# Projections of a hybrid trunk in plain float32 instead of float32r products of split operands, with a ring of 8 weight tiles

## The chip, the cores and the metric

The kernel runs on one NeuronCore of a Trainium2 chip, alone. The metric is the device time of one execution in microseconds (us). Before the change three timed executions took 1420.29, 1420.82 and 1422.03 us; the median is 1420.82 us. The engines are named as the profile names them: PE is TensorE (PEld its weight loads), DVE is VectorE, ACT is ScalarE, POOL is GpSimd, SP is SyncE, which here does little but issue DMAs.

## The reference

One layer on 256 tokens of width 1024, float32 throughout:

```
mod = silu(c) @ ada_w + ada_b                     # 6 x 1024: shift, scale, gate, twice
h   = rmsnorm(x) * (1 + scale1) + shift1
proj = h @ w_in                                   # 1024 x 6688
gdn = 8 heads of a chunked gated delta rule on conv + silu of proj columns, gated, normed
ssd = 16 heads of a chunked state-space scan on conv + silu of proj columns, gated, normed
x   = x + gate1 * (concat(gdn, ssd) @ w_out)      # 2048 x 1024
h   = rmsnorm(x) * (1 + scale2) + shift2
x   = x + gate2 * moe(h)                          # top 4 of 32 experts, each 1024 -> 2 x 1024 -> 1024
out = rmsnorm(x) * final_g
```

## The kernel before

The program has two parts. The **front** does everything up to the router: the vectors of ada_w, the input projection, the delta-rule heads in four pairs (`gdn_pair`), the state-space heads (`ssd`), the output projection, the router. The **expert part** then streams all weights of the 32 experts, 12 loads of 1 MB each, through 20 tiles of 1 MB (`SLOTS`, one tag each; load number n of the stream goes into tag n modulo 20).

In the front the same 20 tiles carry other data. Some are working memory (tags such as g, s1, even, xT), and five, w0 to w4, are the **ring** of weights (`RING`). A unit of the ring is 1 MB: 256 columns of w_in (`Win`, 26 units, the first two before the main loop), 512 columns by 512 rows of w_out (`Wout`, 8 units, which use three tags) or 256 columns of ada_w (`Ada`, 24 units). `issue(tag)` puts the next load into SyncE's queue when its tag is released; loads go in one fixed order and one queue. As the ring empties, `Early` units and `fetch` put the first expert loads into freed tags in the same queue, ahead of later w_out units.

A Win or Wout unit is two **jobs** (`Job`), each 128 columns of w_in (8 products of a 128x128 stationary tile with 256 moving columns, one per 128 rows of depth) or two depth tiles of w_out (4 products of a 128x128 stationary tile with 512 moving columns). A product is not one matmul. `Job.split` first makes a float32r copy of the weights on ACT (`whs`, L323) and the remainder on POOL (`wls`, L327, two halves per job; for the first two units on DVE), one job ahead. The activations are kept as such a pair too (`hs`; for the output projection `ys`, split at L1007 and L1172 on ACT and L1008 and L1173 on DVE). Three float32r matmuls then stand for the float32 product: high x high, high x low, low x high (L363 for Win, L449 for Wout). The weight tile is released right after the split.

A Win job's result lies in one of two PSUM banks of tag mm, from which the convolution reads it: one ACT operation (L538), three DVE operations (L540), then a tanh on ACT and a last DVE operation. The bank is free after the third L540. An Ada unit of the main loop is a chain of eight DVE operations on 128x256 elements (L390, L392). A generator, `fill`, hands out the jobs in halves; `run` mixes those halves into the 27 steps of each `gdn_pair` and the 26 of `ssd`, so that PE has projection work while the heads wait for DVE or ACT. Each engine works through its queue in order.

Chores (loads of biases and of ada_b rows) are issued by POOL, each pinned behind a POOL subtraction of a split.

Of the kernel before, what the change touches and what calls it, by code (L numbers as in the profile page):

```python
# [16 lines left out]
try:  # L17
# [15 lines left out]
KT = D // 128  # L33
# [15 lines left out]
def trunk_kernel(ctx: ExitStack, tc: tile.TileContext, x, c, ada_w, ada_b, norm1_g, norm2_g, w_in,  # L49
# [20 lines left out]
    def slot(tag, name, dt=FT, size=2048):  # L70
        return ring.tile([128, size], dt, name=name, tag=tag, bufs=1)
# [40 lines left out]
    def ts(t):  # L112
        return slice(t * 128, t * 128 + 128)
# [37 lines left out]
    BC = part("s3", 0, [4, SEQ])  # L151
    whs, wls = slot("wh", "whs", FR), slot("wl", "wls", FR)
    nth = {}
# [158 lines left out]
    class Job:  # L312
# [4 lines left out]

        def split(self, dst=None):
            u, i = self.unit, self.i
            w = u.half(i)  # L320
            h = turn("wh") * 1024
            self.wh, self.wl = (v[:, h:h + 1024] for v in dst or (whs, wls))
            self.first = S.activation(u.shaped(self.wh), w, AF.Copy)  # L323
            wh, wl = u.shaped(self.wh), u.shaped(self.wl)
            q = w.shape[1] // 2
            for r in (slice(0, q), slice(q, 2 * q)):
                self.last = (V if dst else G).tensor_tensor(wl[:, r], w[:, r], wh[:, r], op=OP.subtract)  # L327
            if i:
                u.w = None
                issue(u.tag)  # L330

        def mm(self, part):
            self.unit.mm(self, part)

        def post(self):
            self.unit.post(self)

    class Win:
# [8 lines left out]

        def half(self, i):
            return self.w[:, :, ts(i)]

        def shaped(self, v):
            return v.rearrange("p (k m) -> p k m", k=KT)

# [5 lines left out]
        def mm_k(self, job, ks):  # L359
            wh, wl = self.shaped(job.wh), self.shaped(job.wl)  # L360
# [59 lines left out]
    class Wout:  # L420
# [8 lines left out]

        def half(self, i):  # L430
            return self.w[:, 2 * i:2 * i + 2]

        def shaped(self, v):
            return v.rearrange("p (k m) -> p k m", k=2)

        def mm(self, job, t):
            wh, wl = self.shaped(job.wh), self.shaped(job.wl)
# [13 lines left out]

# [22 lines left out]
    def fill():  # L474

        todo, sums, late = None, [], []
        jobs = [j for u in units[KT + 2:] if not isinstance(u, Early) for j in (u.jobs or [u])]
        real = [None] * 4 + [j for j in jobs if isinstance(j, Job)]
        real[4].split()
        n = 4  # L480

        def between():
            if sums:
                try:
                    next(sums[0][0])
                except StopIteration:
                    late.append([1, sums.pop(0)[1]])

        for j in jobs:
            if isinstance(j, Ada):  # L490
                sums.append((j.run(False), j))
# [11 lines left out]
            if n < len(real):  # L503
                real[n].split()
            if n >= 6 and n % 2 == 0 and chores:
                with tc.issue_after(real[n].last.ins):
# [104 lines left out]
    for i, u in enumerate(units[KT:], KT):  # L611
        u.tag = f"w{((i if i < w0 else w0 + (i - w0) % 3) - KT) % RING}"
    for u, i in zip(units, (4, 2, 1, 3, 4, 2, 3, 4)):
        u.tag = f"w{i}"
# [5 lines left out]
    xh = slot("yh", "xh").rearrange("p (t d) -> p t d", t=2)  # L620
    hT = slot("yl", "hT").rearrange("p (k m) -> p k m", k=KT)
    ss1 = fc.tile([128, 2], FT)
# [10 lines left out]

    hs = [slot(tag, "hs", FR).rearrange("p (k m) -> p k m", k=KT) for tag in ("hh", "hl")]
# [5 lines left out]
    wx = [slot(tag, "wx", FR) for tag in ("s2", "g")]  # L640

    def pre_run(i, k):

        for j in pre[2 * i:2 * i + 2]:
            if j.k == 0:
                j.split(wx if i else (whs, wls))
        for j in pre[2 * i:2 * i + 2]:
            j.unit.mm_k(j, range(j.k, k))
            j.k = k

    for k2 in range(KT // 2):
# [70 lines left out]
    wbx = slot("xd", "wbh", FR)  # L722
    wbh = wbx[:, 0:512].rearrange("p (a k m) -> p a k m", a=2, k=KT)
    with tc.issue_after(last[0].ins):
        S.activation(wbh[:, 0], wbd, AF.Copy)
    with tc.issue_after(last[1].ins):
        V.tensor_tensor(wbh[:, 1], wbd, wbh[:, 0], op=OP.subtract)
    p = pg()
    for k in range(KT):
        for j, (a, b) in enumerate(((0, 0), (0, 1), (1, 0))):  # L730
            T.matmul(p[0:32, :SEQ], wbh[:, a, k], hs[b][:, k], start=(k == 0 and j == 0), stop=(k == KT - 1 and j == 2))
    bd = fr.tile([32, 4, 2, 64], FT, name="bd", tag="rot", bufs=3)
# [84 lines left out]
    def gdn_pair(pr):  # L817
# [211 lines left out]
    def gate_chore(dst, c0):  # L1029
        chores.append(lambda: nc.gpsimd.dma_start(dst, ada_b[:, c0:c0 + dst.shape[1]].to_broadcast(list(dst.shape))))  # L1030

    def bias_load(i, src):
        chores.append(lambda: nc.gpsimd.dma_start(bf[32 * i:32 * i + 32], src))

# [31 lines left out]
    def ssd():  # L1066
# [44 lines left out]
        for qd in range(4):  # L1111
# [42 lines left out]
            if qd % 2:  # L1154
# [10 lines left out]
                for t in range(2):  # L1165
                    T.transpose(p[:, ts(t)], rsd[:, t:t + 1].to_broadcast([128, 128]), ident)
                parts_y()
                for ct in range(4 * g, 4 * g + 4):
                    V.scalar_tensor_tensor(xT[:, ct], xT[:, ct], sng[:, ct:ct + 1], p[:, 0:256],
                                           op0=OP.mult, op1=OP.mult)  # L1170
                    yhl = ys[2 + g][:, :, ct % 4]
                    S.activation(yhl[:, 0], xT[:, ct], AF.Copy)  # L1172
                    V.tensor_tensor(yhl[:, 1], xT[:, ct], yhl[:, 0], op=OP.subtract)  # L1173
                yield


    ys = []

    def parts_y():
        ys.append(slot(("yh", "yl")[len(ys) % 2], "ys", FR).rearrange("p (a k m) -> p a k m", a=2, k=4))  # L1180

    parts_y()
    parts_y()
# [405 lines left out]
```

## Time and profile before

| | us |
|---|---|
| median of three timed executions | 1420.82 |
| profiled execution, its own time | 1424.03 |
| its span, first to last instruction | 1422.2 |

The span lies 1.8 us inside the profiled execution's time, and that execution took 3.2 us longer than the median. In the rows further down a busy time is the union of an engine's instructions in a stretch; PEclk is the mean clock that was granted to PE, as a share of full speed (1.00 is 2.4 GHz, 0.50 is 1.2 GHz). A plain float32 matmul of the program stands in the trace as two MATMUL records, a float32r matmul as one. The ends of matmul records are modelled and overlap the next record, so a pace is read from starts and not from durations.

### The profile page before, as it was taken

To read this page: it belongs to the slowest core of one execution; us is meant where nothing else is said; L and a number is where in the kernel's file an instruction comes from. 1 tells how busy PE (TensorE), PEld (TensorE's weight loads), DVE (VectorE), ACT (ScalarE), POOL (GpSimd) and SP (SyncE) were. 2 spreads that over 40 slices of the span, in tenths; PEclk is the share of its full clock that TensorE was granted. 3 is DMA by queue.
4 is the path that set the end of the run, shared out by engine and by line. 5 is a ranking of instruction groups with operands and counts; after the bars stand their busy time and mean duration, and the time that the engine had idled before them with its cause. 6 is when DMAs were issued, how large, how long until landed. Compare 5 with 4: busy or idle time off the path is not lost. (4 is left out here: it accounts for less than half of the span.)

```text
span 1422.2 us, 20287 instructions
## 1 busy us (share of the span) xinstructions
PE 1272.2 (89%) x8024; PEld 662.7 (47%) x8025; DVE 627.0 (44%) x1586; ACT 246.4 (17%) x464; POOL 210.3 (15%) x185
## 2 busy tenths in 40 slices
PE   5889698889888899999999999899998799999996
PEld 3777687788666333333333323233333333333332
DVE  6889998954686322323322322223222133222322
ACT  3343333342243000001000000001000010100001
POOL 3345443444464000000000000000000000000000
PEclk8989898999999999999999999999999899999997
DMA  9754455332628699999999999999999999999990
GB/s 340 240 168 162 155 159 177 110 129 86 240 90 319 276 424 423 422 424 424 424 423 422 424 424 423 423 423 424 424 424 424 424 424 424 381 423 424 422 409 33
DMA packets 130472, 469.78 MB, mean 330 GB/s; under 512 B 7900, under 2 KB 59216, under 8 KB 97568
## 3 DMA queue, kind: packets, MB, share of 16 engines
q1 hardware_dynamic: 128592, 464.58, 81.3%
q8 instruction: 95, 1.56, 0.4%
q0 software_dynamic: 1040, 1.67, 0.4%
q10 hardware_dynamic: 704, 1.64, 0.4%
q14 instruction: 41, 0.34, 0.1%
HBM read 466.22 MB, written 1.05 MB: 329 GB/s over the span
## 5 line engine op out<-in xcount | busy, mean ns | idle before, releaser
L1398 PE MATMUL pG<-w,xe 128*64 128x512 f32 (+1 forms) x1152 | 283.5, 579 | 21.3 <-DMA w<-in_moe_w_gu_dram 21.1
L1398 PE MATMUL pU<-w,xe 128*64 128x512 f32 (+1 forms) x1152 | 280.6, 574 | 0.0
L1426 PE MATMUL pY<-w,hTe 128*64 128x512 f32 x1024 | 225.2, 592 | 0.9 <-ACT hTe L1415 0.7
L1402 DVE TENSOR_SCALAR ga<-pG 128x512 f32<-128x512 f32 (+1 forms) x34 | 23.0, 676 | 411.8 <-PE pG L1398 411.8
L327 POOL TENSOR_TENSOR wls<-w,whs 128x512 fp32r<-128x512 f32 x128 | 170.0, 1350 | 216.5 <-ACT whs L323 205.8
L363 PE MATMUL mm<-hs,whs 128*128 128x256 f32 x800 | 174.1, 310 | 30.7 <-DVE t_c L540 13.1
L1398 PEld LDWEIGHTS pG<-w,xe 128*64 128x64 f32 (+1 forms) x1152 | 83.9, 135 | 163.1 <-issue 103.9
L1398 PEld LDWEIGHTS pU<-w,xe 128*64 128x64 f32 (+1 forms) x1152 | 87.9, 135 | 142.4 <-issue 139.9
L363 PEld LDWEIGHTS mm<-hs,whs 128*128 128x128 f32 x800 | 136.5, 207 | 37.7 <-issue 24.4
L1426 PEld LDWEIGHTS pY<-w,hTe 128*64 128x64 f32 x1024 | 71.8, 137 | 133.0 <-issue 127.9
L363 PE MATMUL mm<-hs,wls 128*128 128x256 f32 x400 | 121.8, 304 | 0.0
L1404 ACT ACTIVATE th<-ga 128x512 f32<-128x512 f32 (+1 forms) x34 | 21.1, 620 | 470.4 <-DVE ga L1402 470.4
L1437 DVE SCALAR_TENSOR_TENSOR ye<-pY,gs,g2p 128x512 f32<-128x512 f32 (+1 forms) x33 | 24.2, 734 | 172.7 <-PEq L1491 163.8
L323 ACT ACTIVATE whs<-w 128x1024 fp32r<-128x1024 f32 x66 | 69.8, 1058 | 84.6 <-PE mm L363 41.7
L363 PEld LDWEIGHTS mm<-hs,wls 128*128 128x128 f32 x400 | 82.8, 207 | 1.6 <-issue 0.7
L392 DVE SCALAR_TENSOR_TENSOR t_c<-w,cact,t_c 128x256 f32<-128x256 f32 x112 | 77.0, 697 | 0.2
L1370 DVE TENSOR_SCALAR xe<-pw,A,sh 128x64 f32<-128x64 f32 (+1 forms) x272 | 70.9, 337 | 0.5 <-PE pw L1366 0.5
L1438 ACT ACTIVATE yh<-ye 128x512 fp32r<-128x512 f32 (+1 forms) x35 | 21.2, 607 | 281.3 <-DVE ye L1437 277.3
L1357 PE MATMUL pw<-xt,P 128*64 128x512 f32 (+1 forms) x288 | 66.0, 592 | 0.0
L1395 PE MATMUL pG<-bias,id 96*64 96x512 bf16 (+1 forms) x72 | 14.6, 394 | 27.7 <-PEq L1491 27.7
L1360 ACT ACTIVATE xg<-pw 128x512 f32<-128x512 f32 (+1 forms) x34 | 19.9, 585 | 110.3 <-PE pw L1357 110.3
L1377 DVE TENSOR_SCALAR QT<-pU 128x256 fp32r<-128x256 f32 x32 | 13.6, 425 | 53.5 <-PE pU L1373 53.4
(444 smaller groups left out, 1345.9 us busy)
## 6 DMA issues: line engine op xcount, KB each, us to landing
w<-in_moe_w_gu_dram SPq DMA_DIRECT2D x256, 1024.0 KB, 19.4
w<-in_moe_w_down_dram SPq DMA_DIRECT2D x127, 1024.0 KB, 19.6
w<-in_w_in_dram SPq DMA_DIRECT2D x26, 1024.0 KB, 5.4
w<-in_ada_w_dram SPq DMA_DIRECT2D x24, 1024.0 KB, 5.3
w<-in_w_out_dram SPq DMA_DIRECT2D x8, 1024.0 KB, 4.8
xt<-in_x_dram ACTq DMA_DIRECT2D x1, 1024.0 KB, 5.3
w<-in_moe_w_down_dram SPq DMA_DIRECT2D x2, 512.0 KB, 17.8
out_dram<-o SPq DMA_DIRECT2D x4, 256.0 KB, 2.0
```

The lines of the kernel that those rows point to most:

```text
L323: self.first = S.activation(u.shaped(self.wh), w, AF.Copy)
L327: self.last = (V if dst else G).tensor_tensor(wl[:, r], w[:, r], wh[:, r], op=OP.subtract)
L363: T.matmul(job.p, a[:, k], hs[b][:, k], start=(k == 0 and j == 0), stop=(k == KT - 1 and j == 2))
L392: V.scalar_tensor_tensor(a, self.w[:, k], cact[:, k:k + 1], a, op0=OP.mult, op1=OP.add)
L1357: T.matmul(p[self.rows(h), :self.wid], self.P[:, t], xt[:, t, self.cols(h)], start=(t == 0), stop=(t == 1))
L1370: V.tensor_scalar(xe[:, k], p[:, c0:c0 + cap], A2[:, k:k + 1], sh2[:, k:k + 1], op0=OP.mult, op1=OP.add)
L1398: self.last = T.matmul(dst, self.xe[:, k], self.w(k)[:, o:o + wid], start=False, stop=(k == KT - 1))
L1402: V.tensor_scalar(ga, self.pG, 7.0, None, op0=OP.min)
L1404: S.activation(th, ga, AF.Tanh, scale=0.851)
L1426: T.matmul(pY[self.rows(n)], self.hT[:, k % self.nt, self.rows(k // self.nt)], self.w(8 + k // 2)[:, k % 2, self.cols(n)], start=False, st ...
L1437: V.scalar_tensor_tensor(ye[:, c], self.pY[:, c], self.gs, g2p[self.cap][:, c], op0=OP.mult, op1=OP.mult)
L1438: S.activation(self.yh[:, c], ye[:, c], AF.Copy)
```

## The change

All products of the two projections, and the small one for beta, alpha and dt (`wbd`), become one plain float32 matmul each, on the loaded weights and the unsplit activations. The splits of weights and activations on ACT, POOL and DVE go. `hT` gets a tag of its own; the tags hh, hl, wh and wl go, and w5, w6 and w7 join the ring, which is now 8 long. A unit's tile is released after its second job's products. Five Early loads instead of two, and then five fetched loads instead of six, come ahead of the fourth w_out unit. The chores go to SyncE's queue.

```
-RING = 5
+RING = 8
-SLOTS = ("w0", "w1", "g", "odd", "c", "hh", "hl", "s2", "s1", "even", "xd", "s3", "w2", "w3", "w4", "wh", "wl", "yh",
+SLOTS = ("w5", "w6", "w7", "w0", "w1", "g", "odd", "c", "hT", "s2", "s1", "even", "xd", "s3", "w2", "w3", "w4", "yh",
          "yl", "xT")
...
-        def split(self, dst=None):
...
-            self.first = S.activation(u.shaped(self.wh), w, AF.Copy)
...
-                self.last = (V if dst else G).tensor_tensor(wl[:, r], w[:, r], wh[:, r], op=OP.subtract)
-            if i:
-                u.w = None
-                issue(u.tag)
         def mm(self, part):
             self.unit.mm(self, part)
+            if part and self.i:
+                self.unit.release()
...
             for k in ks:
-                for j, (a, b) in enumerate(((wh, 0), (wh, 1), (wl, 0))):
-                    T.matmul(job.p, a[:, k], hs[b][:, k], start=(k == 0 and j == 0), stop=(k == KT - 1 and j == 2))
+                T.matmul(job.p, self.w[:, k, ts(job.i)], hT[:, k], start=(k == 0), stop=(k == KT - 1))
...
-                y = ys[self.kp][:, :, k % 4]
-                for j, (a, b) in enumerate(((0, wh), (0, wl), (1, wh))):
-                    T.matmul(oacc[self.nn][t], y[:, a, ts(t)], b[:, i], start=(k == 0 and j == 0),
-                             stop=(k == 15 and j == 2))
+                T.matmul(oacc[self.nn][t], ys[self.kp][:, k % 4, ts(t)], self.w[:, 2 * job.i + i], start=(k == 0),
+                         stop=(k == 15))
...
-            last = (S.activation(hs[0][:, k], hT[:, k], AF.Copy),
-                    V.tensor_tensor(hs[1][:, k], hT[:, k], hs[0][:, k], op=OP.subtract))
...
-        yf = y.rearrange("p c h l -> p (c h l)")
-        V.tensor_tensor(yf, yf, p, op=OP.mult)
-        for hp in range(2):
-            yhl = ys[pr // 2][:, :, pr % 2 * 2 + hp]
-            S.activation(c4(yhl[:, 0]), y[:, :, hp], AF.Copy)
-            V.tensor_tensor(c4(yhl[:, 1]), y[:, :, hp], c4(yhl[:, 0]), op=OP.subtract)
+        V.tensor_tensor(ys[pr // 2][:, pr % 2 * 2:pr % 2 * 2 + 2].rearrange("p h (c l) -> p c h l", c=4), y,
+                        p.rearrange("p (c h l) -> p c h l", c=4, h=2), op=OP.mult)
...
-        chores.append(lambda: nc.gpsimd.dma_start(dst, ada_b[:, c0:c0 + dst.shape[1]].to_broadcast(list(dst.shape))))
+        chores.append(lambda: nc.sync.dma_start(dst, ada_b[:, c0:c0 + dst.shape[1]].to_broadcast(list(dst.shape))))
...
-    fetch(len(W) + 6)
+    fetch(len(W) + 5)
```

The change renumbers the lines: L363, the matmul of Win, is L346 afterwards. The instruction rows below have names like those of the trace; a count after x is of equal instructions in a row.

PE's queue before, after the first two Win units, as the stream of projection matmuls (mm) begins and the product for beta, alpha and dt (the 32x256 rows) is made:

```order
L363 MATMUL mm<-hs,whs 128x256
L731 MATMUL g<-hs,wbh 32x256 x24
L363 MATMUL mm<-hs,whs 128x256
L363 MATMUL mm<-hs,wls 128x256
L363 MATMUL mm<-hs,whs 128x256 x2
L363 MATMUL mm<-hs,wls 128x256
```

PE's queue in the same place of the changed kernel:

```order
L346 MATMUL mm<-hT,w 128x256
L693 MATMUL g<-hT,wbd 32x256 x8
L346 MATMUL mm<-hT,w 128x256 x2
L699 MATMUL g<-ident,bd 128x32 x4
L346 MATMUL mm<-hT,w 128x256 x22
```

One matmul stands where there were three (two with whs, one with wls), here and in every product of the projections; the work of the heads stands between them as before.

POOL's queue before, from the first split on to the middle of the second pair (wls is a remainder of weights; wbh and t_even are the heads' own work; the DMA rows are chores):

```order
L327 TENSOR_TENSOR wls<-w,whs 128x512 x6
L1033 DMA scratch<-in_moe_b_gu_dram 32x1024
L327 TENSOR_TENSOR wls<-w,whs 128x512 x4
L1033 DMA scratch<-in_moe_b_gu_dram 32x1024
L824 TENSOR_TENSOR wbh<-incl_145,gg_630 128x256
L327 TENSOR_TENSOR wls<-w,whs 128x512 x4
L1033 DMA scratch<-in_moe_b_down_dram 32x1024
L327 TENSOR_TENSOR wls<-w,whs 128x512 x4
L1030 DMA g1b<-in_ada_b_dram 128x1024
L327 TENSOR_TENSOR wls<-w,whs 128x512 x4
L897 TENSOR_TENSOR t_even<-t_even,eg 128x512
```

POOL's queue in the changed kernel, all that is left of it in the front from the same point on:

```order
L786 TENSOR_TENSOR wbh<-incl_143,gg_520 128x256 x2
L859 TENSOR_TENSOR t_even<-t_even,eg 128x512
L861 TENSOR_TENSOR t_even<-t_even,eg 128x512
L786 TENSOR_TENSOR wbh<-incl_143,gg_520 128x256
L859 TENSOR_TENSOR t_odd<-t_odd,eg 128x512
L861 TENSOR_TENSOR t_odd<-t_odd,eg 128x512
L786 TENSOR_TENSOR wbh<-incl_143,gg_520 128x256
L859 TENSOR_TENSOR t_even<-t_even,eg 128x512
L861 TENSOR_TENSOR t_even<-t_even,eg 128x512
L859 TENSOR_TENSOR t_odd<-t_odd,eg 128x512
L861 TENSOR_TENSOR t_odd<-t_odd,eg 128x512
L1063 TENSOR_TENSOR ra<-incl,sa_521 128x512 x8
```

128 subtractions and the chores have left the queue; 20 operations of the heads remain.

SyncE's queue before, from the third w_out unit to the fourth (in brackets the semaphores that a load waits for, by engine; DMAHW are earlier loads):

```order
L87 DMA w<-in_w_out_dram 128x4x512 [waits DMAHW2_49,Activation_49,Pool_49]
L87 DMA w<-in_moe_w_gu_dram 128x2048 [waits DMAHW4_49,Activation_49,Pool_49]
L87 DMA w<-in_moe_w_gu_dram 128x2048 [waits DMAHW6_49,Activation_49,Pool_49]
L87 DMA w<-in_moe_w_gu_dram 128x2048 [waits DVE_49,PE_49]
L87 DMA w<-in_moe_w_gu_dram 128x2048 [waits DVE_49] x2
L87 DMA w<-in_moe_w_gu_dram 128x2048 [waits DMAHW7_49,PE_49]
L87 DMA w<-in_moe_w_gu_dram 128x2048 [waits DMAHW0_49]
L87 DMA w<-in_moe_w_gu_dram 128x2048 [waits DMAHW1_49]
L87 DMA w<-in_w_out_dram 128x4x512 [waits DMAHW2_49,Pool_49]
```

And in the changed kernel:

```order
L87 DMA w<-in_w_out_dram 128x4x512 [waits DMAHW6_49,DMAHW3_49,PE_49]
L87 DMA w<-in_moe_w_gu_dram 128x2048 [waits PE_49]
L87 DMA w<-in_moe_w_gu_dram 128x2048 [waits DMAHW7_49,DMAHW5_49,PE_49]
L87 DMA w<-in_moe_w_gu_dram 128x2048 [waits PE_49]
L87 DMA w<-in_moe_w_gu_dram 128x2048 [waits DMAHW0_49,PE_49]
L87 DMA w<-in_moe_w_gu_dram 128x2048 [waits PE_49]
L87 DMA w<-in_moe_w_gu_dram 128x2048 [waits DMAHW1_49,DVE_49]
L87 DMA w<-in_moe_w_gu_dram 128x2048 [waits DMAHW2_49,DVE_49,Pool_49]
L87 DMA w<-in_moe_w_gu_dram 128x2048 [waits DMAHW3_49,DVE_49]
L87 DMA w<-in_moe_w_down_dram 128x2x1024 [waits DMAHW4_49]
L87 DMA w<-in_moe_w_down_dram 128x2x1024 [waits DMAHW5_49]
L87 DMA w<-in_w_out_dram 128x4x512 [waits DMAHW6_49,PE_49]
```

Ten expert loads instead of eight stand ahead of the fourth w_out unit, and where a ring tile was released by ACT and POOL it is now released by PE.

## Rows read from the trace of the kernel before

**Rows 1.** Stretches: length, busy (instructions) of PE, PEld, DVE, ACT, POOL, clock, DMA share, GB/s.
```profile
36.00:52.00 16.00, 16.00 (x145) 14.02 (x144) 9.62 (x25) 5.18 (x11) 3.73 (x4) 1.00 0.89 310
52.00:73.00 21.00, 14.16 (x107) 13.69 (x105) 19.28 (x63) 7.20 (x16) 7.89 (x8) 0.84 0.61 196
73.00:305.00 232.00, 195.73 (x1994) 177.33 (x1994) 202.83 (x442) 85.32 (x169) 110.37 (x91) 0.92 0.46 150
305.00:361.00 56.00, 50.19 (x572) 44.39 (x572) 28.92 (x74) 18.30 (x38) 25.31 (x20) 0.97 0.29 94
361.00:437.00 76.00, 63.02 (x354) 47.29 (x353) 60.33 (x108) 27.54 (x44) 43.08 (x33) 0.96 0.50 188
437.00:451.00 14.00, 13.45 (x71) 10.14 (x69) 7.25 (x14) 5.97 (x16) 8.03 (x6) 1.00 0.75 285
...
476.00:1409.00 933.00, 876.54 (x4560) 330.19 (x4556) 256.80 (x665) 79.04 (x136) 0.00 (x0) 0.99 0.99 410
```

**Rows 2.** SyncE's timeline: start, duration, what was issued.
```profile
439.69 15.96 SPq L87 DMA_DIRECT2D w<-in_moe_w_gu_dram  x8
475.97 5.52 SPq L87 DMA_DIRECT2D w<-in_moe_w_down_dram  x4
```

**Rows 3.** All engines from 154 to 166 us in order of time; in brackets idle before.
```profile
153.91 0.15 DVE L268 TENSOR_TENSOR rot<-roy 128x4 f32<-128x4 f32 x1
...
154.97 5.69 POOL L327 TENSOR_TENSOR wls<-w,whs 128x512 fp32r<-128x512 f32 x4 [6.62 <-ACT whs L323]
...
155.58 1.25 DVE L268 TENSOR_TENSOR rot<-roy 128x4 f32<-128x4 f32 x1
...
161.21 0.47 PE L363 MATMUL mm<-hs,whs 128*128 128x256 f32 x2 [4.47 <-DVE rot L268]
```

**Rows 4.** Single lines: count, duration ns min/median/max, first and last start.
```profile
L392 DVE SCALAR_TENSOR_TENSOR t_c<-w,cact,t_c x112: 387/479/1999, 45.0 to 278.8; 128x256 f32<-128x256 f32 x112
...
L540 DVE SCALAR_TENSOR_TENSOR t_c<-mm,cwg,t_c x72: 465/470/484, 61.3 to 282.6; 128x255 f32<-128x255 f32 x24, 128x254 f32<-128x254 f32 x24, 128x253 f32<-128x253 f32 x24
...
L327 POOL TENSOR_TENSOR wls<-w,whs x128: 1257/1289/1842, 48.3 to 444.4; 128x512 fp32r<-128x512 f32 x128
```

**Rows 5.** The page's groups: count, busy us, mean ns of one, idle before.
```profile
L327 POOL TENSOR_TENSOR wls<-w,whs 128x512 fp32r<-128x512 f32 x128 | 170.0, 1350 | 216.5 <-ACT whs L323 205.8
...
L392 DVE SCALAR_TENSOR_TENSOR t_c<-w,cact,t_c 128x256 f32<-128x256 f32 x112 | 77.0, 697 | 0.2
```

**Rows 6.** PE's waits from 52 to 361 us: in total, times, longest.
```profile
PE mm L363 <- DVE t_c L540: 13.1, 7, 4.0
PE mm L363 <- DVE pl L768: 6.8, 1, 6.8
PE mm L363 <- DVE rot L268: 5.9, 2, 4.5
```

**Rows 7.** PE's timeline at full clock: start, duration, matmuls in a row.
```profile
321.93 0.40 PE L363 MATMUL mm<-hs,whs 128*128 128x256 f32 x2
...
322.29 0.40 PE L363 MATMUL mm<-hs,whs 128*128 128x256 f32 x2
...
364.09 0.63 PE L449 MATMUL iv<-whs,ys 128*128 128x512 f32 x2
...
364.79 0.62 PE L449 MATMUL iv<-whs,ys 128*128 128x512 f32 x2
...
376.94 1.88 PE L1096 MATMUL g<-xe,t_s 128*128 128x512 f32 x4
```

**Rows 8.** Line L1096 alone: duration ns min/median/max, first and last start.
```profile
L1096 PE MATMUL g<-xe,t_s x4: 590/592/592, 376.9 to 378.2; 128*128 128x512 f32 x4
```

**Rows 9.** Stretches, PE and PEld of L363 alone; last of L449 alone.
```profile
73.00:305.00 232.00, 136.33 (x855) 118.42 (x855) 0.92 0.46 150
305.00:361.00 56.00, 33.29 (x214) 27.78 (x215) 0.97 0.29 94
...
361.00:437.00 76.00, 40.45 (x151) 28.47 (x152) 0.96 0.50 188
```

More of the change, by code (lines that the diff above doesn't have):

```diff
@@ L316, in __init__ @@
             self.unit, self.i = unit, i
-        def split(self, dst=None):
[L319 to L322, printed above, removed]
-            self.first = S.activation(u.shaped(self.wh), w, AF.Copy)
-            wh, wl = u.shaped(self.wh), u.shaped(self.wl)
-            q = w.shape[1] // 2
-            for r in (slice(0, q), slice(q, 2 * q)):
-                self.last = (V if dst else G).tensor_tensor(wl[:, r], w[:, r], wh[:, r], op=OP.subtract)
-            if i:
-                u.w = None
-                issue(u.tag)
         def mm(self, part):
             self.unit.mm(self, part)
+            if part and self.i:
+                self.unit.release()
         def post(self):
@@ L346, in load, with release @@
             self.w = load(win_src[:, :, self.c0:self.c0 + 256], [KT, 256], self.tag, self in loads[:10])
[L348 to L352, printed above, removed]
+        def release(self):
+            self.w = None
+            issue(self.tag)
         def mm(self, job, part):
@@ L359, in mm_k @@
         def mm_k(self, job, ks):
-            wh, wl = self.shaped(job.wh), self.shaped(job.wl)
             for k in ks:
-                for j, (a, b) in enumerate(((wh, 0), (wh, 1), (wl, 0))):
-                    T.matmul(job.p, a[:, k], hs[b][:, k], start=(k == 0 and j == 0), stop=(k == KT - 1 and j == 2))
+                T.matmul(job.p, self.w[:, k, ts(job.i)], hT[:, k], start=(k == 0), stop=(k == KT - 1))
         def post(self, job):
@@ L428, in load, with release @@
             self.w = load(wout_src[:, 4 * self.kp:4 * self.kp + 4, self.nn * 512:self.nn * 512 + 512], [4, 512], self.tag, True)
[L430 to L434, printed above, removed]
+        def release(self):
+            self.w = None
+            issue(self.tag)
         def mm(self, job, t):
-            wh, wl = self.shaped(job.wh), self.shaped(job.wl)
             k0 = 4 * self.kp + 2 * job.i
@@ L477, in fill @@
         jobs = [j for u in units[KT + 2:] if not isinstance(u, Early) for j in (u.jobs or [u])]
-        real = [None] * 4 + [j for j in jobs if isinstance(j, Job)]
-        real[4].split()
         n = 4
@@ L502, in fill @@
             n += 1
-            if n < len(real):
-                real[n].split()
             if n >= 6 and n % 2 == 0 and chores:
-                with tc.issue_after(real[n].last.ins):
+                with tc.issue_after(last_load[0].ins):
                     chores.pop(0)()
@@ L612, in trunk_kernel @@
         u.tag = f"w{((i if i < w0 else w0 + (i - w0) % 3) - KT) % RING}"
-    for u, i in zip(units, (4, 2, 1, 3, 4, 2, 3, 4)):
+    for u, i in zip(units, (2, 3, 4, 5, 6, 7, 2, 3)):
         u.tag = f"w{i}"
@@ L620, in trunk_kernel @@
     xh = slot("yh", "xh").rearrange("p (t d) -> p t d", t=2)
-    hT = slot("yl", "hT").rearrange("p (k m) -> p k m", k=KT)
+    hT = slot("hT", "hT").rearrange("p (k m) -> p k m", k=KT)
     ss1 = fc.tile([128, 2], FT)
@@ L631, in trunk_kernel @@
         issue(f"w{i}")
-    hs = [slot(tag, "hs", FR).rearrange("p (k m) -> p k m", k=KT) for tag in ("hh", "hl")]
     pre = [j for u in units[KT:KT + 2] for j in u.jobs]
@@ L639, in trunk_kernel @@
         j.p, j.k = p[:, :SEQ], 0
-    wx = [slot(tag, "wx", FR) for tag in ("s2", "g")]
     def pre_run(i, k):
-        for j in pre[2 * i:2 * i + 2]:
-            if j.k == 0:
-                j.split(wx if i else (whs, wls))
         for j in pre[2 * i:2 * i + 2]:
@@ L649, in pre_run @@
             j.k = k
+        if k == KT:
+            j.unit.release()
     for k2 in range(KT // 2):
@@ L722, in trunk_kernel @@
     wbx = slot("xd", "wbh", FR)
[L723 to L727, printed above, removed]
     p = pg()
     for k in range(KT):
-        for j, (a, b) in enumerate(((0, 0), (0, 1), (1, 0))):
-            T.matmul(p[0:32, :SEQ], wbh[:, a, k], hs[b][:, k], start=(k == 0 and j == 0), stop=(k == KT - 1 and j == 2))
+        T.matmul(p[0:32, :SEQ], wbd[:, k], hT[:, k], start=(k == 0), stop=(k == KT - 1))
     bd = fr.tile([32, 4, 2, 64], FT, name="bd", tag="rot", bufs=3)
@@ L1029, in gate_chore @@
     def gate_chore(dst, c0):
-        chores.append(lambda: nc.gpsimd.dma_start(dst, ada_b[:, c0:c0 + dst.shape[1]].to_broadcast(list(dst.shape))))
+        chores.append(lambda: nc.sync.dma_start(dst, ada_b[:, c0:c0 + dst.shape[1]].to_broadcast(list(dst.shape))))
     def bias_load(i, src):
-        chores.append(lambda: nc.gpsimd.dma_start(bf[32 * i:32 * i + 32], src))
+        chores.append(lambda: nc.sync.dma_start(bf[32 * i:32 * i + 32], src))
     def bias_part(j):
@@ L1166, in ssd @@
                     T.transpose(p[:, ts(t)], rsd[:, t:t + 1].to_broadcast([128, 128]), ident)
-                parts_y()
                 for ct in range(4 * g, 4 * g + 4):
-                    V.scalar_tensor_tensor(xT[:, ct], xT[:, ct], sng[:, ct:ct + 1], p[:, 0:256],
+                    V.scalar_tensor_tensor(ys[2 + g][:, ct % 4], xT[:, ct], sng[:, ct:ct + 1], p[:, 0:256],
                                            op0=OP.mult, op1=OP.mult)
-                    yhl = ys[2 + g][:, :, ct % 4]
-                    S.activation(yhl[:, 0], xT[:, ct], AF.Copy)
-                    V.tensor_tensor(yhl[:, 1], xT[:, ct], yhl[:, 0], op=OP.subtract)
                 yield
     ys = []
[L1179 to L1183, printed above, removed]
+    for tag in ("yh", "yl"):
+        v = slot(tag, "ys").rearrange("p (q k m) -> p q k m", q=2, k=4)
+        ys += [v[:, 0], v[:, 1]]
     for pr in range(4):
         run(gdn_pair(pr), (20, 32, 44, 52)[pr], 27)
-    fetch(len(W) + 6)
+    fetch(len(W) + 5)
     V.scalar_tensor_tensor(A2, A2, 1.0, col("n2", 8), op0=OP.add, op1=OP.mult)
```

1 line of the change is left out of this document (removed).

## The prediction

> **What bounds the kernel now.** I first read the stretches of the trace by engine, from the end backwards. From 476 to 1409 us the DMA engines are 0.99 busy and PE 876.54 of 933 us [rows 1]: the expert part waits for weights. Nothing in it changes, so the change can only move its beginning. That beginning stands in SyncE's timeline: the last 8 loads of the first filling of the 20 tiles are issued by 439.69 + 15.96 = 455.65 us, and the next load goes out at 475.97 us [rows 2], when the first expert's products release a tile. Between them SyncE waits for PE, so a front that ends earlier by some microseconds moves the stream, and the end, by as many, as long as the filling is done by then.
>
> Then the front, stage by stage [rows 1]. PE is busy 14.16 of 21 us (0.67), 195.73 of 232 (0.84), 50.19 of 56 (0.90), 63.02 of 76 (0.83) and 13.45 of 14 us (0.96). DVE is busy 19.28 of 21 and 202.83 of 232 us, then only 28.92 of 56. So up to 305 us both engines are nearly full, and from 305 us on PE leads. The granted clock is 0.84 and 0.92 in the first two stages: part of the time PE runs at 1.2 and not at 2.4 GHz.
>
> Third, why is DVE so full? The chain of Ada (L392) has a median of 479 ns, a mean of 697 and a maximum of 1999 ns for one shape [rows 4, 5]. The convolution (L540), of nearly the same shape but with one operand in PSUM, never leaves 465 to 484 ns. One place shows what happens: a 128x4 operation takes 0.15 us at 153.91 us, and 1.25 us at 155.58 us, while POOL runs its subtractions for 5.69 us; PE then idles 4.47 us until DVE comes through [rows 3]. The waits of PE give the price: ahead of L363 alone 13.1 + 6.8 + 5.9 us end with a DVE instruction, the middle one a single wait of 6.8 us [rows 6].
>
> **The change part by part.** *PE, price of a product.* At full clock three float32r matmuls with 256 columns take 322.29 - 321.93 = 0.36 us, with 512 columns 364.79 - 364.09 = 0.70 us [rows 7]. Plain float32 with 512 columns: 4 records, two products, in 1.88 us of which the last record's 0.59 us are one duration, so (1.88 - 0.59) / 3 = 0.43 us a record and 0.86 us a product [rows 7, 8]. For 256 columns no row exists. Exactly half of it, 0.43, is the low end; four paces of a float32r record, 4 x 0.12 = 0.48, the high end. Float32r records fall from 0.70 / 3 = 0.233 to 0.12 with the columns, a ratio of 1.94, so I take 0.86 / 1.94 = 0.44. A product then costs 0.08 us more in the input projection and 0.16 us more in the output projection.
>
> The Trainium skill states in "FP8 and Floating Point Precision", TensorE Precision Notes, that true float32 takes four passes through the array, against three here. At the float32r pace that would be 0.48 and 0.93 us; the row with 512 columns has 0.86, so the trace bears out the number of passes and not that price. What it would do is the third rival below.
>
> *Count.* 26 units of two jobs of 8 products are 416: 855 / 3 = 285 in 73 to 305 us, 214 / 3 = 71 in 305 to 361 [rows 9], and the other 60 before 73 us, about 27 of them in 52 to 73. The output projection has 8 x 2 x 4 = 64, of which 151 / 3 = 50 before 437 us [rows 9] and 14 after. Extra PE work: 2.6 + 2.2 + 22.8 + 5.7 + 8.0 + 2.2 = 43.5 us.
>
> *What PE gets back.* POOL loses 128 subtractions, 170.0 us [rows 5], and with them goes the reason for DVE's long operations. By L392 alone that is (697 - 479) x 112 = 24 us of DVE, and every small operation of the heads that now waits is shortened too. DVE also loses the subtractions that split activations; I count those as nothing, since DVE is not the bound afterwards. POOL's 20 operations that stay still meet DVE, mostly in the state-space heads.
>
> The Trainium skill's page "SBUF — State Buffer", Who interferes with whom, says that a DVE instruction with two SBUF inputs and a POOL instruction that reads SBUF exclude each other, and that whichever issues first keeps the port while the other blocks. By that rule the loss could as well lie with POOL, and then removing its work would free nothing on DVE. The rows decide: L327 stays near 1289 ns at a minimum of 1257, while L392 goes up to 1999 [rows 4]; it is DVE that waits.
>
> *The sum.* PE's work at full clock is its busy time times the granted clock, plus the extra work. The stage is that work over the busy share that PE then reaches. For the three stages up to 361 us I take 0.92, between the 0.90 of the stage where PE already leads (it still has waits under POOL's subtractions) and the 0.96 of 437 to 451; for the state-space stage 0.90, for its own chains of waits stay.
> - 52 to 73 us: 14.16 x 0.84 + 2.2 = 14.1; / 0.92 = 15.3: -5.7 us.
> - 73 to 305: 195.73 x 0.92 + 22.8 = 202.9; / 0.92 = 220.5: -11.5.
> - 305 to 361: 50.19 x 0.97 + 5.7 = 54.4; / 0.92 = 59.1: +3.1.
> - 361 to 437: 63.02 x 0.96 + 8.0 = 68.5; / 0.90 = 76.1: +0.1.
> - 437 to 451: +2.2 in full, for the last w_out units follow the last head output.
> - Before 52 us PE is busy 16.00 of 16 us from 36 on [rows 1], so nothing hides the extra work there: +2, less 0.6 that falls into the waits for ada_w before.
>
> Together -9.8 us. The profiled execution would take 1424.03 - 9.8 = 1414.2 us; it lies 3.2 us above the median, so against that I forecast **1411 us**.
>
> *SyncE's queue.* The chores are 10 more issues there with no wait but that for earlier loads, hidden by a ring that is eight deep. Ten instead of eight expert loads stand before the fourth w_out unit, each waiting for its tile; five of them follow Win units that PE finishes one after another. A w_out tile is now freed by its products instead of its split, some 3 us a job later. Six loads are left for the end instead of eight: at 410 GB/s [rows 1] 6.3 MB take 15 us, and 476 - 451 = 25 us are there. I count this as nothing; without that cover it costs what the 15 us exceed the 25 by.
>
> **The rivals.** *PE is not handed back its idle time (slower).* The heads' chains of small steps PE - DVE - ACT - PE could set the pace in 73 to 437 us, whatever POOL does: only some 26 us of PE's idle time there are waits ahead of L363 [rows 6], and DVE stays well used. With the full clock but the old shares 0.67, 0.84, 0.90, 0.83 the stages take 21.0, 241.5, 60.4 and 82.5 us: 0 + 9.5 + 4.4 + 6.5 + 3.6 = +24, that is 1445 us. It decides from one common share of PE over 52 to 437 us: (14.1 + 202.9 + 54.4 + 68.5) / (385 - 3.6) = 0.89; below it the kernel is slower, and it was 323.1 / 385 = 0.84 before. Against it speaks that the longest idle times end right after POOL's.
>
> *Everything is handed back (faster still).* With 0.96 in all four stages: 14.7, 211.4, 56.7 and 71.4 us: -6.3 - 20.6 + 0.7 - 4.6 + 3.6 = -27, 1394 us. For it: 361 to 451 shows PE full when its inputs are there. Against: DVE's remaining work and the heads' chains.
>
> *The product costs 0.48 and 0.93 us (slower).* 383 x 0.04 / 0.92 + 33 x 0.04 + 64 x 0.07 = 22 us on top: 1433 us. The row with 512 columns speaks against it; none excludes it for 256. The Trainium skill's four passes in "FP8 and Floating Point Precision" would give this price if each took what a float32r record takes.
>
> *The front moves and the end doesn't.* If the last loads came 10 us later than reckoned, the stream would begin when the tiles are full: 1421 us, no change. SyncE's idle 20 us before 475.97 [rows 2] speak against it.
>
> **How the numbers follow.** The forecast with shares from 0.90 to 0.95 has a chance of 0.54 (1397 to 1418 us), the larger gain 0.11, no change 0.11 (the last rival, or shares just at 0.89), the slow chains 0.17, the dear product 0.07. A measurement of this kernel can tell 0.2%, 2.8 us, from no change. Faster: 0.54 + 0.11 = 0.65; same 0.11; slower 0.24. The range 1391 to 1435 leaves out about 0.1 above, the worse half of the slow chains, and less than 0.1 below. The forecast's own range is 1397 to 1418.
>
> **What would show it.** L392 with a mean near its median and no 128x4 operation over 0.3 us outside POOL's 20 operations; the waits ahead of the Win matmuls under 8 us in all; a clock over 0.96 from 73 to 305 us; plain float32 with 256 columns at 0.22 us a record; the first load of the second filling about 10 us earlier than 475.97 us and the same 933 us after it. The forecast is wrong if DVE's waits go and PE's share in 73 to 437 us still stays under 0.89, or if the record's pace is over 0.24 us.

## The result, and the profile after

The changed kernel takes **1373.6 us** (median of 4 runs, 1371.7 to 1375.7) against 1420.7 for the kernel before. The ratio is 0.966, with an interval from 0.965 to 0.968: 47 us faster. I had forecast 1411 us with a range down to 1391. The sign and the way were right, and the size was off by a factor of nearly five. The profiled run took 1375.7 us, with a span of 1373.9 us.

The stretches first; the columns are those of [rows 1]: length, busy (instructions) of PE, PEld, DVE, ACT, POOL, clock, DMA share, GB/s. The bounds are about the same places in the program by the count of the input projection's products, which now come earlier.

```profile
36.00:52.00 16.00, 16.00 (x101) 12.57 (x99) 5.67 (x15) 1.53 (x4) 0.00 (x0) 0.99 0.78 264
52.00:71.00 19.00, 19.00 (x93) 14.54 (x93) 17.85 (x75) 5.30 (x17) 0.62 (x1) 1.00 0.93 316
71.00:267.00 196.00, 194.62 (x1698) 157.99 (x1697) 155.38 (x431) 49.69 (x126) 10.42 (x9) 1.00 0.58 189
267.00:321.00 54.00, 53.93 (x517) 43.14 (x516) 24.41 (x75) 10.37 (x28) 2.49 (x2) 1.00 0.23 80
321.00:391.00 70.00, 69.45 (x304) 37.13 (x303) 40.38 (x96) 10.56 (x20) 8.48 (x8) 1.00 0.56 216
391.00:402.00 11.00, 11.00 (x46) 5.96 (x45) 4.24 (x12) 3.25 (x12) 0.00 (x0) 1.00 0.41 157
427.00:1361.00 934.00, 875.93 (x4560) 330.69 (x4555) 256.48 (x664) 78.92 (x136) 0.00 (x0) 0.99 0.99 410
```

Compare the first busy column with the length, line by line: PE is busy 194.62 of 196 us, 53.93 of 54, 69.45 of 70, where [rows 1] have 195.73 of 232, 50.19 of 56, 63.02 of 76. From 52 us on the clock column says 1.00, that is 2.4 GHz throughout, where it said 0.84 and 0.92. The last line is the expert part, 934 us as before.

SyncE's timeline shows the place where a gain of the front becomes a gain of the kernel, as in [rows 2]: start, duration, what was issued.

```profile
379.83 27.86 SPq L87 DMA_DIRECT2D w<-in_moe_w_gu_dram  x8
426.64 5.52 SPq L87 DMA_DIRECT2D w<-in_moe_w_down_dram  x4
```

The first load of the second filling is at 426.64 instead of 475.97 us, 49.3 us earlier. The first filling has been issued by 379.83 + 27.86 = 407.69, 19 us before, so it is still the first expert's products that release the stream.

In the timeline of all engines, the counterpart of [rows 3], the same small operations of DVE:

```profile
140.79 0.15 DVE L267 TENSOR_TENSOR rot<-roy 128x4 f32<-128x4 f32 x1
...
141.20 0.15 DVE L268 SCALAR_TENSOR_TENSOR rot<-rot,vv 128x4 f32<-128x4 f32 x1
...
142.69 1.97 PE L346 MATMUL mm<-hT,w 128*128 128x256 f32 x8 [0.25 <-DVE rot L268]
...
142.93 0.15 DVE L269 SCALAR_TENSOR_TENSOR roy<-rot,roy 128x4 f32<-128x4 f32 x1
```

Each takes 0.15 us. PE's wait for them, 4.47 us before, is 0.25 us. The single lines (ns min/median/max, first and last start) answer to [rows 4]; L375 is the former L392, L514 the former L540:

```profile
L375 DVE SCALAR_TENSOR_TENSOR t_c<-w,cact,t_c x112: 466/479/487, 47.6 to 199.7; 128x256 f32<-128x256 f32 x112
...
L514 DVE SCALAR_TENSOR_TENSOR t_c<-mm,cwg,t_c x72: 462/477/485, 61.7 to 244.0; 128x255 f32<-128x255 f32 x24, 128x254 f32<-128x254 f32 x24, 128x253 f32<-128x253 f32 x24
```

The Ada chain's maximum went from 1999 to 487 ns. The convolution, which never was held up, is as it was. All waits of PE between 52 and 402 us that the trace names (in total, times, longest), for [rows 6]:

```profile
PE iv L883 <- DVE t_s L877: 1.0, 1, 1.0
PE g L1099 <- DVE t_s L1082: 0.3, 1, 0.3
PE mm L346 <- DVE rot L268: 0.2, 1, 0.2
PE g L964 <- DVE roy L269: 0.2, 1, 0.2
```

Ahead of the Win matmuls alone there were 13.1 + 6.8 + 5.9 us, now 0.2. Last, PE's timeline for the price of a product, for [rows 7]:

```profile
138.82 3.62 PE L346 MATMUL mm<-hT,w 128*128 128x256 f32 x16
...
335.02 3.60 PE L427 MATMUL mm<-w,ys 128*128 128x512 f32 x8
```

The last of the 16 records lasts 0.38 us, so one takes (3.62 - 0.38) / 15 = 0.216 us and a product of two records 0.43. With 512 columns, where the last record lasts 0.59, it is (3.60 - 0.59) / 7 = 0.43, and 0.86 a product. I had put 0.44 and 0.86.

### The profile page after: what moved, and what is told of

It is laid out like the page before. It is cut to its first block, busy times and chain, and to the rows that moved or that the text cites. A ratio compares the mean times of both kernels' runs of the same rounds, so it can differ in the third digit from the quotient of the medians.

```text
span 1373.9 us, 18891 instructions
## 1 busy us (share of the span) xinstructions
PE 1284.3 (93%) x7536; PEld 627.9 (46%) x7537; DVE 541.8 (39%) x1553; ACT 172.2 (13%) x371; POOL 33.9 (2%) x47
## 5 line engine op out<-in xcount | busy, mean ns | idle before, releaser
L346 PE MATMUL mm<-hT,w 128*128 128x256 f32 x800 | 202.3, 392 | 0.2 <-DVE rot L268 0.2
L346 PEld LDWEIGHTS mm<-hT,w 128*128 128x128 f32 x800 | 144.2, 192 | 21.9 <-issue 3.7
L375 DVE SCALAR_TENSOR_TENSOR t_c<-w,cact,t_c 128x256 f32<-128x256 f32 x112 | 52.6, 479 | 0.8
L514 DVE SCALAR_TENSOR_TENSOR t_c<-mm,cwg,t_c 128x255 f32<-128x255 f32 (+2 forms) x72 | 34.4, 477 | 7.0 <-ACT t_c L512 6.6
L1402 PE MATMUL acc<-yh,QT 64*128 64x512 f32 (+1 forms) x148 | 33.4, 430 | 3.2 <-ACT yh L1390 3.2
L1347 PEld LDWEIGHTS <-id 96*64 96x64 bf16 (+1 forms) x144 | 6.0, 108 | 61.0 <-PEq L1443 57.0
L1309 PEld LDWEIGHTS pw<-xt,P 128*64 128x64 f32 (+1 forms) x288 | 17.1, 135 | 30.9 <-issue 30.1
```

The costliest lines, as they stand in the source:

```text
L346: T.matmul(job.p, self.w[:, k, ts(job.i)], hT[:, k], start=(k == 0), stop=(k == KT - 1))
L375: V.scalar_tensor_tensor(a, self.w[:, k], cact[:, k:k + 1], a, op0=OP.mult, op1=OP.add)
L514: V.scalar_tensor_tensor(acc[:, s:], p[:, :SEQ - s], wc(3 - s), acc[:, s:], op0=OP.mult, op1=OP.add)
L1309: T.matmul(p[self.rows(h), :self.wid], self.P[:, t], xt[:, t, self.cols(h)], start=(t == 0), stop=(t == 1))
L1402: T.matmul(dst, self.QT[n % 2][half_, t], part[half_, i * w:(i + 1) * w], start=False, stop=part is self.yl, skip_group_check=True)
```

## The experiments

Three theories stood against each other on where PE's time came from. **L**: POOL's subtractions lock DVE out, and taking them away gives DVE and PE their time back. **A**: it is ACT's copies, or the number of steps that a split adds, that hold the front up. **W**: the longer products do it, because more matmul time per step of the heads hides DVE's chains. Each run is compared with runs of the kernel before on the same chip. Line numbers differ from kernel to kernel; in the cuts of code, ... marks what is left out.

**chores_sp.** The kernel before with only the queue change: the ten chores (three loads of biases, seven of ada_b rows) go out on SyncE, behind the last weight load, and not behind a subtraction on POOL's queue. The kernels without subtractions need it, since they have none to hang the loads on.

```
-  with tc.issue_after(real[n].last.ins):
+  with tc.issue_after(last_load[0].ins):
...
-  chores.append(lambda: nc.gpsimd.dma_start(dst, ada_b...
+  chores.append(lambda: nc.sync.dma_start(dst, ada_b...
...
```

> The kernel before with one part of the change: the chores (bias loads and ada_b rows) are issued by SyncE behind its latest load instead of by POOL behind a subtraction. Every theory: no change, 1417 to 1424 us; POOL's part in them is 13 issues of some 0.5 us. A gain of over 5 us would make the chores a cause of its own. It is the base for the next three runs.

1427.8 us, ratio 1.005 (1.003 to 1.007). I had expected no change, and 1424 us at most; this part of the change gains nothing and costs 0.5%. The whole gain lies in the rest.

**no_pool_sub.** chores_sp without POOL's subtractions; the third matmul reads the high part again, so PE's work stays and the result lacks the weights' low part:

```
...
-  self.last = (V if dst else G).tensor_tensor(wl[:, r], w[:, r], wh[:, r], op=OP.subtract)
+  self.wl = self.wh
```

> As chores_sp, but the remainder of the weights is left out: no subtraction on POOL (nor on DVE for the first two units), and the third float32r matmul reads the high part again, so PE has the same matmuls and the result lacks the low part of the weights. Theory L (POOL's subtractions hold up DVE, and that alone makes PE idle and its clock fall in the front): PE's work at full clock from 52 to 451 us was 315 us of 399; at a share of 0.92 to 1.00 that is 342 to 315 us, so 1337 to 1364 us. Theory A (copies on ACT that wait for PE hold up the convolution's ACT operations queued behind them): 1405 to 1425 us. Theory W (PE stays busy in the changed kernel only because a plain float32 product is longer work per step of the heads): PE idles as before, 1410 to 1425 us.

1355.4 us, ratio 0.954 (0.950 to 0.958): theory L. The front, 52 us to the end of the output projection, of the kernel before and then of no_pool_sub:

```profile
52.00:451.00 399.00, 336.55 (x3091) 292.83 (x3088) 318.61 (x700) 144.32 (x280) 194.69 (x156) 0.93 0.46 157
```

```profile
52.00:377.00 325.00, 313.56 (x3092) 276.94 (x3090) 242.64 (x693) 142.28 (x276) 22.66 (x20) 0.98 0.56 194
```

The same number of matmul records to within one, and 74 us less. The third busy column is DVE: 318.61 became 242.64 us for nearly the same instructions (700 and 693), so some 76 us of DVE's "busy" time was waiting inside its instructions. The Ada chain alone accounts for a third of it (77.0 us in [rows 5], 52.3 here); the rest is in the many small operations.

**no_act_copy** and **no_split.** ACT's copy runs only once per buffer, so later products use an old high part; in no_split POOL's subtractions go as well.

```
-  self.first = S.activation(u.shaped(self.wh), w, AF.Copy)
+  if fresh:
+      self.first = S.activation(u.shaped(self.wh), w, AF.Copy)
```

> As chores_sp, but the high part of the weights is copied on ACT once for each buffer and then used stale, so ACT's 66 copies all but go, while POOL's subtractions stay; the result is of wrong weights. Theory L: within 8 us of chores_sp, 1412 to 1428 us. Theory A: 1365 to 1390 us. Theory W: 1412 to 1428 us.

> As chores_sp, but both parts are made once for each buffer and then used stale: neither copies on ACT nor subtractions on POOL, three float32r matmuls per product as before; the result is of wrong weights, and most w_in and w_out loads are waited for by nobody. It shows what float32r products would take if splitting were free. Theory L: within 8 us of no_pool_sub, 1330 to 1364 us. Theory A: within 8 us of no_act_copy. Theory W: 1410 to 1425 us.

1428.8 us, ratio 1.005 (1.003 to 1.008), the same as chores_sp: theory A falls as far as ACT's copies go; the number of steps is taken up by sub_on_dve below. Without both it is 1351.4 us, ratio 0.950 (0.947 to 0.954), and no_pool_sub already has nearly all of that. In the front it has all of it: the last matmul of the output projection starts at 376.5 us in no_split and at 376.7 in no_pool_sub. The kernels' times differ by more because what comes after the front is not the same work once the weights are wrong. From the front's end to the end of the kernel, in the kernel before, no_pool_sub and no_split:

```profile
451.00:1422.20 971.20, 897.99 (x4644) 342.11 (x4642) 276.22 (x756) 85.59 (x152) 0.00 (x0) 0.97 0.97 402
```

```profile
377.00:1354.30 977.30, 907.59 (x4889) 350.44 (x4888) 283.19 (x779) 87.58 (x158) 0.00 (x0) 0.98 0.96 398
```

```profile
377.00:1350.10 973.10, 900.15 (x4646) 342.66 (x4644) 276.10 (x756) 85.75 (x154) 0.00 (x0) 0.98 0.96 400
```

no_pool_sub runs 245 matmul records more there and takes 6 us longer than the kernel before (four_passes, below, has the same count and takes 10 us longer). The program has extra steps for an expert that is given more than 64 tokens, so other weights can mean other work; that this is the reason is not shown. The front is the better measure for these kernels.

**after_pool.** The other direction: the changed kernel, and POOL again subtracts two 128x512 halves for each job of the input projection, into a part of a tile that is free at that time, 96 subtractions in all. The products stay plain float32.

```
+  w, o = self.unit.w[:, :, ts(self.i)], wbx[:, 0:512]...
+  for r in (slice(0, 4), slice(4, 8)):
+      G.tensor_tensor(o, w[:, r], w[:, r], op=OP.subtract)
```

> The changed kernel with POOL's load put back for the input projection: two subtractions of 128x512 per job on the job's own weights, w - w into an unused tile, one job ahead as before; nobody reads them, but a weight tile is released after them too. Output as in the changed kernel. Theory L: DVE is held up as before, PE idles and its clock falls; with the dearer products that gives 1400 to 1440 us. Theory W (longer work per step keeps PE busy whatever DVE does): 1372 to 1385 us. Theory A: 1372 to 1380 us, since ACT's copies stay away.

1408.5 us, ratio 0.992 (0.990 to 0.994): 35 of the 47 us are gone. Theory W, as a rival to L, falls: the longer products don't hide the chains while POOL subtracts. Its front, and its Ada chain:

```profile
52.00:434.00 382.00, 357.13 (x2640) 263.91 (x2641) 279.73 (x683) 78.85 (x199) 123.48 (x110) 0.96 0.49 166
```

```profile
L382 DVE SCALAR_TENSOR_TENSOR t_c<-w,cact,t_c x112: 466/479/1330, 46.6 to 222.8; 128x256 f32<-128x256 f32 x112
```

PE is busy 357.13 of 382 us, at a mean of 0.96 of the full clock. The matmuls are those of the changed kernel, some 348 us of work at full clock, and 348 / 382 is a share of 0.91. The chain has its long instructions back.

**after_memset.** Is it any work of POOL, or its reading from SBUF? The changed kernel with four memsets of 128x512 per job in place of those subtractions; a small copy on ACT, which waits for the memsets of the job before, paces them:

```
+  S.activation(tiny, o[:, 0:1], AF.Copy)
+  for r in range(4):
+      G.memset(o, 0.0)
```

> The kernel after, with GpSimd kept as busy as before during the input projection, but with work that reads nothing from SBUF: four memsets of 128x512 per job, about 2.2 us a job. Theory P (it is GpSimd's reading from SBUF that shuts VectorE out): the time stays, 1371 to 1383, and the Ada chain stays at 479 ns. Theory G (any work of GpSimd beside VectorE does it): as with the spare subtractions of after_pool, 1395 or more, with the Ada chain's maximum over 1000 ns.

1378.3 us, ratio 0.969 (0.965 to 0.972). The front, and the Ada chain:

```profile
52.00:407.00 355.00, 351.54 (x2664) 260.95 (x2663) 247.22 (x688) 85.04 (x239) 101.04 (x168) 1.00 0.53 179
```

```profile
L384 DVE SCALAR_TENSOR_TENSOR t_c<-w,cact,t_c x112: 465/478/575, 47.1 to 205.3; 128x256 f32<-128x256 f32 x112
```

POOL is busy 101 us in the front, not far from the 123 of after_pool. The memsets run ahead of the jobs and end at 160 us, so the fair comparison is the stretch up to there, in the changed kernel, after_pool and after_memset:

```profile
52.00:160.00 108.00, 107.46 (x832) 87.18 (x831) 94.72 (x294) 30.35 (x81) 7.74 (x7) 1.00 0.73 239
```

```profile
52.00:160.00 108.00, 95.88 (x688) 76.11 (x689) 100.60 (x246) 23.46 (x62) 49.41 (x43) 0.94 0.65 212
```

```profile
52.00:160.00 108.00, 106.41 (x809) 85.69 (x808) 94.54 (x287) 33.86 (x113) 82.62 (x151) 1.00 0.69 224
```

With POOL busy 82.62 of 108 us on memsets, DVE's busy time is 94.54 us against 94.72 without them, and PE's 106.41 against 107.46; with only 49.41 us of POOL, but subtractions, PE falls to 95.88 at 0.94 of the clock. Writing alone disturbs the front hardly at all. The 5 us by which this front ends later arise mostly ahead of 52 us, where PE waits 4.0 us for ACT, whose small copies wait 60.2 us in all for memsets. One kind of DVE operation does get longer, the first of each Ada chain, with one large input in SBUF (the changed kernel, then after_memset):

```profile
L373 DVE TENSOR_SCALAR t_c<-w,cact x16: 338/346/353, 47.2 to 189.7; 128x256 f32<-128x256 f32 x16
```

```profile
L382 DVE TENSOR_SCALAR t_c<-w,cact x16: 336/387/773, 46.7 to 195.3; 128x256 f32<-128x256 f32 x16
```

There are only 16 of these in the front's main loop, so it costs little here.

The rule in the Trainium skill, "SBUF — State Buffer", Who interferes with whom, names exactly this pair, a DVE instruction with two SBUF inputs against a POOL instruction that reads SBUF. The two Ada rows (maximum 1330 and 575 ns) agree with it, and so does the convolution in [rows 4], which has an operand in PSUM and never went over 484 ns.

**sub_on_dve.** chores_sp with the split whole, but all subtractions on DVE, so that the number of steps stays:

```
-  self.last = (V if dst else G).tensor_tensor(...
+  self.last = V.tensor_tensor(...
```

> The kernel before (float32r kept, the chores on SyncE as in chores_sp) with all subtractions of the weights' remainders on VectorE instead of GpSimd. Theory L (GpSimd's subtractions hold VectorE up): the long operations of VectorE go, worth up to the 74 us that leaving the remainder out took off the front, but VectorE gets 128 operations of about 0.69 us, 88 us, and it was full already; 1375 to 1405, between the two kernels. The Ada chain goes back to a mean of about 479 ns. Rival A (it is ScalarE's copies, semaphores or the mere number of steps that hold the front up): the steps are all still there and VectorE has more to do, so 1415 or more.

1406.2 us, ratio 0.990 (0.987 to 0.994), one microsecond over the span that I gave to L, and under what A needs (1415 or more). The front, and what PE waits for most:

```profile
52.00:435.00 383.00, 335.91 (x3085) 288.89 (x3082) 316.96 (x817) 143.42 (x275) 23.58 (x20) 0.94 0.48 162
```

```profile
PE mm L363 <- DVE wls L327: 8.2, 15, 1.8
```

DVE's busy time is 316.96 us, against 318.61 with the subtractions on POOL. Handing 128 subtractions to POOL had freed DVE of nothing: they add 316.96 - 242.64 = 74 us to its busy time in the front, and it had lost 76 us waiting. The Ada chain does not come back wholly, as I had expected: its mean is 504 ns and not 479, with a maximum of 1587, while POOL's 20 other operations are still there.

**four_passes.** Does PE now set the front alone? no_pool_sub with a fourth float32r matmul in every product of both projections (the input projection's is shown), the price of my third rival:

```
-  for j, (a, b) in enumerate(((wh, 0), (wh, 1), (wl, 0))):
+  for j, (a, b) in enumerate(((wh, 0), (wh, 1), (wl, 0), (wl, 1))):
```

> no_pool_sub (no subtraction of weights on GpSimd, the remainder left out and the high part in its place) with a fourth float32r matmul per product, so that a product costs 0.48 and 0.93 us, the price of the third rival. It adds 383 x 0.12 + 64 x 0.23 = 61 us of TensorE work to the 309 that no_pool_sub has between 52 and 377 us. Theory F (once the lock is gone, TensorE's work over a share of 0.99 sets the front): 370 / 0.99 = 374 us, the front ends at 426, 1399 to 1408; the step from the kernel after, whose work is 348, is then one for one. Rival S (TensorE keeps the share 0.96 of no_pool_sub, since the chains between the engines stay): 370 / 0.96 = 385, 1412 to 1420.

1400.8, 1406.2 and 1408.2 us in three runs, ratio 0.988 (0.984 to 0.992); a fourth run of 5724 us, whose cause is unknown, is left out of it. The front decides for theory F, which had its end at 426 us:

```profile
52.00:425.00 373.00, 370.86 (x3569) 333.58 (x3568) 251.13 (x703) 146.02 (x284) 22.37 (x20) 1.00 0.50 170
```

PE has 370.86 of 373 us, a share of 0.994, and from the changed kernel's 348 us of work to 371 the front ends 402 -> 425 us: one for one.

**after_ring5.** The changed kernel with a ring of 5 instead of 8:

```
-RING = 8
+RING = 5
```

> The changed kernel with a ring of 5 again: w5, w6 and w7 wait for the expert loads from the start, behind w0 and w1 in their order. Theory L, A and W: within 4 us of the changed kernel, 1370 to 1378 us, for no PE wait of the front was put down to a weight load. Theory R (the deeper ring, with tiles that are now held until their products, is part of the gain): 1382 us or more, with waits for w_in loads ahead of the Win matmuls.

1376.7 us, ratio 0.969 (0.966 to 0.972): the longer ring is worth some 3 us, and since the intervals of the two kernels overlap even that is not clear of noise.

**mixed**, an attempt at a faster version: since PE is full and DVE no longer is, every second job of the main loop's input projection is split again, with the subtraction on DVE and a ring of 5.

```
...
+  S.activation(wh, w, AF.Copy)
+  for r in (slice(0, 4), slice(4, 8)):
+      V.tensor_tensor(wl[:, r], w[:, r], wh[:, r], op=OP.subtract)
```

> The kernel after with a ring of 5 weight tiles; every second job of the input projection in the main loop is split again, but with the subtraction on VectorE and none on GpSimd: a copy by ScalarE, two subtractions of 128x512 by VectorE, three float32r matmuls per product. Theory L: the lock is not back, and TensorE, which is 0.99 busy up to 402 us, loses 24 jobs x 8 products x 0.07 us = 14 us of work; the ring of 5 costs up to 3 us; 1361 to 1374. Rival D (VectorE, which gets 33 us more, sets the pace again): 1376 or more, with TensorE idle ahead of the Win matmuls.

1384.4 us, ratio 0.973 (0.970 to 0.977), 8 us more than after_ring5 and not the 3 to 16 us less that L asked for: rival D. The stretch of the heads, and PE's longest waits:

```profile
71.00:267.00 196.00, 183.33 (x1770) 156.95 (x1768) 169.03 (x457) 62.12 (x136) 12.40 (x9) 0.96 0.55 174
```

```profile
PE mm L356 <- DVE ws L322: 4.1, 2, 2.7
PE mm L356 <- DVE roy L269: 3.9, 1, 3.9
PE mm L356 <- DVE rot L268: 2.1, 1, 2.1
```

PE has less to do, and stands idle 12.7 us in this stretch (1.4 in the changed kernel), and its clock falls to 0.96. At 169 of 196 us DVE's chains arrive late again. No kernel here that computes the whole reference beats the changed one.

## Why the prediction was wrong

**What bounds the kernel: right.** The expert part is a stream of weights that only its beginning moves. That came 49.3 us earlier, and from it to the span's end there are 947.3 us (1373.9 - 426.64), against 946.2 before.

**Why DVE was full: right, and shown.** no_pool_sub and after_pool say that it was POOL's subtractions, taken out and put back; no_act_copy and sub_on_dve that it was neither ACT's copies nor the steps; after_memset that it was not POOL's work as such. That it is a subtraction's reading from SBUF rests on this one contrast with memsets. "It is DVE that waits" was too simple, though: POOL's subtractions went up to 1842 ns over a minimum of 1257 in [rows 4], and those of after_pool from 1034 to 2120, so POOL waits too, and it does not matter there.

**The price of a product: right.** 0.43 and 0.86 us against 0.44 and 0.86. The trace shows two records a product, so the four passes that I called borne out are not to be seen in it; the price is. The dear product, my third rival, was no matter of the chip; four_passes shows what it would have cost.

**PE's work: a little too high.** Between 52 us and the end of the output projection PE's busy time times the clock went from 313 to 348 us. My sum has 355.5 at the places of the five stages. Of the 7.5 us too many, 383 x 0.01 = 4 are the 0.44; the rest I can't place.

**The busy share: the step that failed.** I divided that work by 0.92 in the three stages up to 361 us and by 0.90 up to 437. PE reached 348.0 of 350, 0.994, all at full clock. By my lines the five stages take 399 - 11.8 = 387.2 us. With 0.994 under my own sum of 355.5 they take 357.6: 29.6 us of the miss. The 7.5 us of work make up the rest down to the 350 measured. With the 2 us that I had added ahead of 52 us (about 33 products of the input projection have been made there before and after, so the count shows no delay; its line says 2 less 0.6, and the total took 2), this is 39.2 of the 39.5 us between -9.8 and -49.3.

Where the 0.92 came from shows the mistake. I took it between the 0.90 of 305 to 361 us and the 0.96 of 437 to 451, as the stages "where PE already leads". But in both POOL was at work, 25.31 of 56 and 8.03 of 14 us by [rows 1], nearly all of it on subtractions. I had just named those subtractions as the cause of PE's idle time, and then read the ceiling from stretches that still had them. after_pool makes it plain: with the subtractions left in, PE's share is 0.91 and the kernel takes 1408 us. My 1411 is, but for 3 us, the time of a kernel that keeps most of what the change removes; that its share is near mine is no accident, that the two times are so close is in part chance.

Two things lift the share, and the runs part them in the main. Without the lock, and with the old products, PE's work of 309 us (with the clock taken stretch by stretch; 313.56 x 0.98 gives 307) takes 325 us, a share of 0.95. The longer products then fill what is left: 39 us more work lengthen the front by only 25 us (377 to 402), and beyond that, as in four_passes, each microsecond counts whole. four_passes says the same without any other change: 62 us more work than no_pool_sub (371 against 309) lengthen its front by 48. So theory W had a part after all, some 14 us, but only once the lock was gone. In the length of the front: POOL's subtractions cost 74 us (451 against 377), and plain float32 takes 25 of them back, which leaves the 49 that were measured.

**The queue: right.** Nothing waited for SyncE in a way that the end shows; the chores alone cost 7 us in the kernel before (chores_sp), where the front still had the lock, and in the changed kernel PE is busy 0.994 of the front, so they can cost little there. Why they cost that much there I did not follow up.

**The rivals.** "Everything is handed back" was the right one in kind; I had given it 0.11, and even it had 0.96 for a ceiling. The slow chains, decided at a common share of 0.89, did not come: it is 0.994. The front moved and the end moved with it.

**What would show it.** Every mark came as written (the Ada mean, no 128x4 operation of L267 to L269 over 0.17 us, waits under 8 us, the clock, 0.22 us a record, the same length after the first load) except the one on size: 49 and not 10 us earlier.

## What to carry to other kernels

When you have named the cause of an idle time, take the share that follows its removal from a stretch in which that cause is absent, or say that there is none and let the range reach to 1.00. An engine's "busy" time may be waiting inside its instructions: compare the minimum, median and maximum of one shape before calling an engine full. Work handed to GpSimd that reads SBUF was not free for VectorE here; ask what it costs there before asking what it saves. And when a test kernel computes something else, compare the part that the test is about: what follows may no longer be the same work.

## What the runs showed of the hardware

The size of the exchange between the two engines was not expected: 128 subtractions of 128x512, 170 us of POOL [rows 5], cost DVE 76 us, as much as they add to its busy time when they run on DVE itself (74 us in sub_on_dve). A 128x4 operation became eight times as long (0.15 and 1.25 us in [rows 3]). POOL memsets of the same tile size, 0.53 us each, did not have this effect (94.54 against 94.72 us of DVE's time in the same 108 us), but for the operation with one input in SBUF, which went from 353 to 773 ns at most. And plain float32 with 256 columns is two records of 0.216 us per product, 0.43, against 0.36 for three float32r matmuls: on PE the split saves a sixth, less than what making its parts on another engine costs here.
